# A hybrid transformer backbone on one core: no elementwise work on GpSimd in RWKV, a quota of products, source order on three engines, and weights two tiles ahead

## Chip, core and metric

The kernel runs on one core of a Trainium2 chip. The metric is the device time of one execution in microseconds (us); the time before is the median of three runs. The engines are TensorE (PE, with its weight loads PEld), VectorE (DVE), ScalarE (ACT), GpSimd (POOL) and SyncE (SP), which issues most transfers (DMAs); ScalarE issues some on a queue of its own (ACTq). Each engine runs its own instructions in order, and semaphores make one wait for another.

## The reference

Two layers work on 256 latent tokens and 256 context tokens of width 1024. Each is a feed-forward half step, three token mixers on one projection, and another feed-forward half step. Cut to what matters:

```python
z = _modulate(x, norm_g, m[3], m[4]) @ w_in             # all mixers' inputs and the gates zg
ya = attention(za)                                       # mixer A
yl = (lru(xl, forward) + lru(xl, reverse)) * gelu(ug)    # mixer B: gated linear recurrence
yr = head_groupnorm(o_forward + o_reverse + bonus) * gate  # mixer C: RWKV-7
g = sigmoid(zg)                                          # three gates of width 1024
acc = g[0] * (ya @ proj[0]) + g[1] * (yl @ proj[1]) + g[2] * (yr @ proj[2])
x = x + m[5] * (acc @ w_out)
```

RWKV runs, for each head and direction, `s = s * w + sa x (kk * a) + v x k`, with `sa = s . (-kk)`, over all tokens. In layer 1 only the latent half of the output is needed.

## The kernel before

Everything is float32. A product of weights is done in three parts: the weight tile (128 x 1024 of the matrix, loaded as `wr` on SP's queue) is cast to a short high half `wh` on ScalarE, the rest `wl = wr - wh` is subtracted on VectorE, and the input is split the same way (`h_hi`, `h_lo`, or `yh`, `yl`). `gemm_steps` then issues, for each of 8 blocks of 128 rows, the three products high x high, high x low and low x high: 24 products a tile, 512 columns each in layer 0 and 256 in layer 1 for the gates. `wload` does load, cast and subtraction in one go. In the stages named `r0` and `r1` a quarter of each tile's subtraction goes to GpSimd (`POOL_PART`).

The change lies in these two stages, about 600 to 1117 us (layer 0) and 2105 to 2560 us (layer 1). There, mixers B (`lru`) and C (`rwkv`) run beside the products of the rest of `w_in` (8 tiles for mixer B, 24 for the gates; `tiles`) and then the projections of branches 0 and 1 (`branch`, 96 products each): 960 products in all. `rwkv` works on four pairs of heads, called heads 0 to 3 here. Each goes through `direction` (decays, keys, and transposes `pt`), `decay`, `invert` (line 1160 begins it with the transposes `XZ`; `pq`, `pz`, `pm` and `pw` are its products), and `back` (`values`, `recur`).

The class `Weave` writes the order of PE. Each part is a generator that yields a `step` with its estimated cost on PE, VectorE, ScalarE and GpSimd and with what it needs. `run` keeps a model time: it takes the first part that is ready, and when none is, or PE was busy too little lately, it calls `fill` for one more product. The order of PE is that of the source in these stages (`manual_schedule`); the order on VectorE, ScalarE, GpSimd and SP is found by a scheduler, which may put an instruction far ahead of its place in the source.

`tiles` loads the tile after the present one before it issues the present one's products. A gate tile ends with a tanh on ScalarE (`gt`), stored to `gd`. `branch` loads its input in four tiles `yr` on ScalarE's queue (line 1450) and splits each as it comes (`yh` on ScalarE at line 231, `yl` on VectorE); `yr` has one buffer in layer 0 and two in layer 1. It then loads weights of `branch_proj` and the gates `gr` (line 1459, ScalarE's queue), issues products `bp`, and adds into `acc`. The transfer of `x` back from memory (line 1489, 2 MB in layer 0) is on ScalarE's queue too.

Of the kernel before, what the change touches and what calls it, by code (L numbers as in the profile page):

```python
# [8 lines left out]
F32 = mybir.dt.float32  # L9
# [18 lines left out]
HOP, BACKLOG, WINDOW, ACTIVE, PERIOD = 0.25, 1.5, 3.4, 3.3, 50.0  # L28
# [6 lines left out]
POOL_PART = {'r0': 0.25, 'r1': 0.25}  # L35
# [60 lines left out]
def build(tc, a, out, upto=99, dbg=None):  # L96
# [3 lines left out]
    with es:  # L100
# [90 lines left out]
        def wload(src, kt=KD, slot=None):  # L191

            n = wn[0]
# [4 lines left out]
            nc.sync.dma_start(out=view(raw), in_=src.rearrange("(k p) c -> p k c", p=P))  # L200
            if slot is None:
# [530 lines left out]
        class Weave:  # L732
# [13 lines left out]
            def products(self):  # L746
                if not self.fill(1):
                    return False
                self.busy(*self.product)
# [8 lines left out]
            def run(self, *parts):  # L758
# [4 lines left out]
                while at:  # L763
# [12 lines left out]
                    if best is None or (low and best[2][0]) or (wanted and self.t > self.owed):  # L776
                        if self.products():
# [5 lines left out]
                    pe, area, eng, lag, need = best[2]  # L783
                    self.busy(pe, area)
# [11 lines left out]
            owed = 0.0  # L796
# [4 lines left out]
        def lru(l, yd, done):  # L801
# [8 lines left out]
            def first(set_):  # L810
# [30 lines left out]
                for f in range(4):  # L841
# [4 lines left out]
                    yield step(dve=2.1, act=0.65, need=[("x", f)] + [("scanned", f - 2)] * (f > 1))  # L846
# [10 lines left out]
                    for d in range(2):  # L857
# [10 lines left out]
                        yield step(dve=0.7, act=1.95, pool=1.6)  # L868
                        nc.scalar.activation(tg[1], tg[1], AF.Identity, bias=one)
                        nc.gpsimd.tensor_tensor(bb[:, d], tg[1], xc, ALU.mult)  # L870
# [3 lines left out]
                    yield step(dve=1.4, act=1.3, pool=0.7, need=[("u", f)])  # L874
# [4 lines left out]
                    nc.gpsimd.tensor_scalar(w, w, 0.044715, 1.0, ALU.mult, ALU.add)  # L879
# [6 lines left out]
            def second(set_):  # L886
                for f in range(4):
# [3 lines left out]
                    for d in range(2):  # L891
                        yield step(pool=1.6, lag=1 - d)
                        nc.gpsimd.tensor_tensor(bb[:, d], th[:, d], bb[:, d], ALU.mult)
                    for d in range(2):
                        yield step(dve=1.3, lag=2)
# [8 lines left out]
                    yield step(dve=0.7, pool=1.6)  # L904
                    y = lp.tile([P, T], F32, tag="yl", name=f"yl{l}{f}", bufs=1)
                    nc.gpsimd.tensor_tensor(y[:, qc:], th[:, 0, qc:], th[:, 1, qc:], ALU.add)
# [44 lines left out]
        def rwkv(l, rk, z, zd, yd, weave, beside, before_last):  # L951
# [7 lines left out]
            with ExitStack() as ey:  # L959
# [4 lines left out]
                hv = rx.tile([P, 28], F32, tag="hv28", name=f"hv{l}")  # L964
                st, Y = {}, {}

                def setup():
# [7 lines left out]
                    nc.vector.tensor_scalar(hv[:, 24:28], hv[:, 20:24], -1.0, 1.0, ALU.mult, ALU.add)  # L975
                    nc.scalar.activation(twd, twd, AF.Tanh)
# [10 lines left out]
                    yield step(dve=4.5, act=0.4)  # L987
# [55 lines left out]
                def direction(f, d):  # L1043
                    nm = f"{l}{f}"

                    yield step(dve=1.22, pool=0.62, lag=0, need=[("tw", f)])
# [22 lines left out]
                    yield step(dve=1.4, pool=1.6 * d, lag=0, need=[("one", f)] * d + [("loaded", f)] * (f > 1))  # L1069
# [22 lines left out]
                def bonus(f):  # L1092

                    nm = f"{l}{f}"
                    yield step(dve=0.75, pool=1.15, lag=0, need=[("both", f)])
                    bon = st[f][4][0]

                    nc.gpsimd.tensor_copy(seg3(k_[f]), step_view(v_[f], 1))
# [28 lines left out]
                def decay(f, d):  # L1127

                    nm = f"{l}{f}"
                    yield step(pool=1.9, lag=0, need=[("paired", f, d)])  # L1130
# [252 lines left out]
                def finish(fs, pool):  # L1383

                    yield step(dve=4.5, act=0.4)
# [258 lines left out]
```

## Time and profile before

| what | value |
|---|---|
| median of three runs | 2797.81 us (2794.79 to 2802.01) |
| the profiled execution | 2800.25 us, its span 2798.4 us |
| mean granted clock of TensorE | 0.94 |
| PE busy | 2629.1 us (94%) |
| DVE busy | 1730.3 us (62%) |
| ACT busy | 1058.6 us (38%) |
| POOL busy | 406.7 us (15%) |

The span reaches from the first instruction to the last, and the time of the execution is a little longer. A busy share is a mean over the whole program: PE's 94% holds long stretches without a gap, and the two stages of the change, which hold most of the rest.

### The profile page before, as it was taken

What the parts mean: (1) busy time and instruction counts of PE and PEld (TensorE: products, weight loads), DVE (VectorE), ACT (ScalarE), POOL (GpSimd) and SP (SyncE); (2) the same over time, 40 slices, a digit from 0 to 9 for tenths busy, and PEclk for the clock granted to TensorE, in tenths of its full rate; (3) what the DMA queues carried; (4) which work ended last, traced back from release to release, by engine and by line L of the source; (5) the groups of instructions that cost most, each with busy time, mean ns of one, the idle gap of its engine ahead of it and who ended that gap; (6) DMA issues with size and microseconds to landing.
All of it is one profiled execution on the core that took longest, in us unless ns stands there. A gap on an engine that the chain in (4) does not pass through costs nothing. (4 is left out here: it accounts for less than half of the span.)

```text
span 2798.4 us, 47830 instructions
## 1 busy us (share of the span) xinstructions
PE 2629.1 (94%) x19761; PEld 2186.4 (78%) x19761; DVE 1730.3 (62%) x2934; ACT 1058.6 (38%) x1673; POOL 406.7 (15%) x381
## 2 busy tenths in 40 slices
PE   7999999997999999899999999999998899887899
PEld 5788888765677776798888978888776788777899
DVE  5867557657666644766655674555657656646565
ACT  4323233335544432332323432324346544333343
POOL 1000002224311102300000100001134432113000
PEclk9999999998898979999999999999999897768999
DMA  7646433122221125735443464544224331026465
GB/s 268 211 151 188 139 98 110 57 80 68 65 65 41 52 82 181 243 91 151 145 119 97 153 194 155 170 153 119 74 78 126 86 90 53 4 78 179 125 184 159
DMA packets 480092, 341.85 MB, mean 122 GB/s; under 512 B 17307, under 2 KB 448884, under 8 KB 479618
## 3 DMA queue, kind: packets, MB, share of 16 engines
q1 hardware_dynamic: 460690, 314.22, 37.2%
q10 hardware_dynamic: 19120, 24.52, 3.0%
q8 instruction: 155, 2.54, 0.4%
q14 instruction: 63, 0.52, 0.1%
q0 software_dynamic: 64, 0.05, 0.0%
HBM read 318.56 MB, written 20.19 MB: 121 GB/s over the span
## 5 line engine op out<-in xcount | busy, mean ns | idle before, releaser
L206 ACT CAST wh<-wr 128x1024 fp32r<-128x1024 f32 (+2 forms) x434 | 436.3, 1008 | 1079.0 <-PE gu L222 360.0
L215 DVE TENSOR_TENSOR wl<-wr,wh 128x1024 fp32r<-128x1024 f32 (+3 forms) x404 | 462.8, 1147 | 307.2 <-ACT wh L206 292.1
L222 PE MATMUL gu<-h_hi,wh 128*128 128x512 f32 (+1 forms) x1528 | 535.7, 352 | 6.2 <-ACT h_hi L388 2.6
L222 PE MATMUL gu<-h_hi,wl 128*128 128x512 f32 (+1 forms) x1528 | 534.0, 350 | 1.8 <-DVE wl L215 1.8
L222 PE MATMUL gu<-h_lo,wh 128*128 128x512 f32 (+1 forms) x1528 | 534.3, 350 | 0.7 <-DVE h_lo L389 0.5
L222 PE MATMUL win<-h_hi,wl 128*128 128x512 f32 (+1 forms) x896 | 335.0, 374 | 16.6 <-DVE wl L215 16.6
L222 PE MATMUL win<-h_hi,wh 128*128 128x512 f32 (+1 forms) x896 | 334.5, 374 | 1.1 <-ACT wh L206 0.6
L222 PE MATMUL win<-h_lo,wh 128*128 128x512 f32 (+1 forms) x896 | 332.6, 371 | 0.0
L222 PEld LDWEIGHTS gu<-h_hi,wh 128*128 128x128 f32 x1528 | 290.7, 191 | 49.8 <-ACT wh L206 6.3
L222 PEld LDWEIGHTS gu<-h_hi,wl 128*128 128x128 f32 x1528 | 291.4, 191 | 40.1 <-DVE wl L215 3.3
L222 PEld LDWEIGHTS gu<-h_lo,wh 128*128 128x128 f32 x1528 | 291.3, 191 | 37.5 <-DVE h_lo L389 1.5
L280 DVE SCALAR_TENSOR_TENSOR adacc<-adw,sc,adacc 128x1024 f32<-128x1024 f32 x196 | 245.1, 1286 | 6.0 <-ACT adacc L278 2.7
L222 PEld LDWEIGHTS win<-h_hi,wl 128*128 128x128 f32 x896 | 181.1, 202 | 57.4 <-issue 19.5
L222 PEld LDWEIGHTS win<-h_lo,wh 128*128 128x128 f32 x896 | 180.9, 202 | 36.6 <-issue 16.4
L222 PEld LDWEIGHTS win<-h_hi,wh 128*128 128x128 f32 x896 | 181.7, 203 | 32.6 <-issue 11.8
L222 PE MATMUL dn<-gh,wh 128*128 128x512 f32 (+1 forms) x560 | 200.8, 359 | 0.0
L222 PE MATMUL dn<-gl,wh 128*128 128x512 f32 (+1 forms) x560 | 199.4, 356 | 0.1
L222 PE MATMUL dn<-gh,wl 128*128 128x512 f32 (+1 forms) x560 | 199.4, 356 | 0.0
L214 POOL TENSOR_TENSOR wl<-wr,wh 128x256 fp32r<-128x256 f32 (+1 forms) x88 | 91.4, 1039 | 331.9 <-ACT wh L206 244.8
L290 POOL MEMSET adrow<- 128x256 f32 x18 | 5.6, 313 | 840.2 <-PE adt L297 840.2
L471 DVE SCALAR_TENSOR_TENSOR x<-dn,cf,x 128x256 f32<-128x256 f32 x120 | 53.6, 480 | 113.1 <-PE dn L222 112.8
L505 DVE TENSOR_TENSOR th<-th,gu 128x512 f32<-128x512 f32 (+1 forms) x88 | 54.4, 619 | 110.6 <-PE gu L222 110.4
(557 smaller groups left out, 4449.6 us busy)
## 6 DMA issues: line engine op xcount, KB each, us to landing
wr<-ffn_w_gu SPq DMA_DIRECT2D x176, 512.0 KB
adw<-ada_w SPq DMA_DIRECT2D x144, 512.0 KB
wr<-w_in SPq DMA_DIRECT2D x106, 512.0 KB
wr<-ffn_w_d SPq DMA_DIRECT2D x64, 512.0 KB
wr<-ffn_w_d SPq DMA_DIRECT2D x35, 384.0 KB
wr<-w_out SPq DMA_DIRECT2D x17, 512.0 KB
gd<-gt SPq DMA_DIRECT2D x24, 256.0 KB
wr<-branch_proj SPq DMA_DIRECT2D x24, 256.0 KB
```

The source lines that it names most:

```text
L206: nc.scalar.copy(hi[:, 0:w], raw[:, 0:w])
L214: nc.gpsimd.tensor_tensor(lo[:, m:w], raw[:, m:w], hi[:, m:w].bitcast(F32), ALU.subtract)
L215: eng.tensor_tensor(lo[:, 0:m], raw[:, 0:m], hi[:, 0:m].bitcast(F32), ALU.subtract)
L222: nc.tensor.matmul(ps[:, c0:c1], wt[:, k], xt(k)[:, c0:c1], start=(k == 0 and j == 0), stop=(k == kt - 1 and j == 2))
L280: nc.vector.scalar_tensor_tensor(acc, w, f, acc, ALU.mult, ALU.add)
L290: nc.gpsimd.memset(row, 0.0)
L471: nc.vector.scalar_tensor_tensor(x[:, k, cs], ps[:, cs], coef[:, s, k:k + 1], x[:, k, cs], ALU.mult, ALU.add)
L505: nc.vector.tensor_tensor(th[:, c0:], th[:, c0:], pp[1][:, c0:], ALU.mult)
```

## The change

The change has four parts, all of them in the two stages.

1. *GpSimd.* All elementwise work of the stages leaves GpSimd: the quarter of `wl` and the operations on `bb`, `yl`, `km` go to VectorE (the first, `bb`, as one fused operation, for which ScalarE loses an addition), and `gl`, `tw`, the copy of `v` and the decay go to ScalarE, the decay as eight activations of 128 columns. Memsets stay.
2. *Quota.* `Weave` refuses a product when more than 960 x (0.08 + steps / 390) are sent, unless one is wanted. The modelled hop is 0.3 instead of 0.25 us, and the costs of some steps are new.
3. *Order.* `manual_schedule` covers VectorE and ScalarE as well: their instructions stand as the source has them, the transfers that ScalarE issues included.
4. *Transfers.* `tiles` fetches a tile of `w_in` two tiles ahead; its cast and subtraction stand after product 9 of 24 of the tile before. `branch` is not changed.

```diff
-HOP, BACKLOG, WINDOW, ACTIVE, PERIOD = 0.25, 1.5, 3.4, 3.3, 50.0
+HOP, BACKLOG, WINDOW, ACTIVE, PERIOD = 0.3, 1.5, 3.4, 3.3, 50.0
+STEPS, PRODUCTS, AHEAD = 390, 960, 0.08
-POOL_PART = {'r0': 0.25, 'r1': 0.25}
+POOL_PART = {}
...
-            def products(self):
+            def products(self, wanted=False):
+
+                if not wanted and self.sent > PRODUCTS * (AHEAD + self.steps / STEPS):
+                    return False
                 if not self.fill(1):
                     return False
+                self.sent += 1
...
-                        nc.scalar.activation(tg[1], tg[1], AF.Identity, bias=one)
-                        nc.gpsimd.tensor_tensor(bb[:, d], tg[1], xc, ALU.mult)
+                        nc.vector.scalar_tensor_tensor(bb[:, d], tg[1], 1.0, xc, ALU.add, ALU.mult)
...
-                    nc.gpsimd.tensor_scalar(w, w, 0.044715, 1.0, ALU.mult, ALU.add)
+                    nc.scalar.activation(w, w, AF.Identity, bias=one, scale=0.044715)
...
-                        nc.gpsimd.tensor_tensor(bb[:, d], th[:, d], bb[:, d], ALU.mult)
...
+                        nc.vector.tensor_tensor(bb[:, d], th[:, d], bb[:, d], ALU.mult)
...
-                    nc.gpsimd.tensor_tensor(y[:, qc:], th[:, 0, qc:], th[:, 1, qc:], ALU.add)
+                    nc.vector.tensor_tensor(y[:, qc:], th[:, 0, qc:], th[:, 1, qc:], ALU.add)
...
-                    nc.gpsimd.tensor_scalar(tw, tw, -0.5 * E05, -0.5 * E05, ALU.mult, ALU.add)
+                    nc.scalar.activation(tw, tw, AF.Identity, bias=hv[:, 28:29], scale=-0.5 * E05)
...
-                        nc.gpsimd.tensor_tensor(seg3(bon)[:, s0:], seg3(bon)[:, s0:], step_view(km, 1)[:, s0:], ALU.add)
+                        nc.vector.tensor_tensor(seg3(bon)[:, s0:], seg3(bon)[:, s0:], step_view(km, 1)[:, s0:], ALU.add)
...
-                    nc.gpsimd.tensor_copy(seg3(k_[f]), step_view(v_[f], 1))
+                    nc.scalar.copy(seg3(k_[f]), step_view(v_[f], 1))
...
-                    nc.gpsimd.tensor_tensor(bkT[:, d], bkT[:, d], pc[:, d, :, None].to_broadcast([P, NCH, P]), ALU.mult)
+                    for j in range(NCH):
+                        nc.scalar.activation(bkT[:, d, j], bkT[:, d, j], AF.Copy, scale=pc[:, d, j:j + 1])
...
+            fetch = lambda t: t and wfetch(a["w_in"][l][:, t[0] * P:(t[0] + 1) * P])
+            now, then = following(), following()
+            w, raw = wsplit(fetch(now)), fetch(then)
             while now:
                 i, c0, key = now
-                now = following()
-                wn_ = load(now[0]) if now else None
+                last = following()
+                ahead = fetch(last)
...
+                for n, _ in enumerate(gemm_steps(ps, w, lambda k: h_hi[:, k], lambda k: h_lo[:, k], KD, c0)):
+                    yield
+                    if n == 8 and then:
+                        wn_ = wsplit(raw)
...
-                with tc.manual_schedule(engines={mybir.EngineType.PE}):
+                with tc.manual_schedule(engines={mybir.EngineType.PE, mybir.EngineType.DVE, mybir.EngineType.Activation}):
```

`wfetch` is the first half of `wload` (the transfer), `wsplit` the second (cast and subtraction). In the following rows, a row is a line, an operation and `output<-inputs`; the numbers are those of the program's tiles.

ScalarE in layer 0, where branch 0 is prepared, before: `gt` is a gate's tanh, `yr` a load, `yh` its cast, `gr` a load of a gate.

```order
L1436 ACTIVATE gt_8959<-win_48_8861 128x512
L1450 DMA yr_9399<-yd_3754 128x512
L1273 COPY W_6333<-pu_8977 64x512 x2
L1273 COPY W_6333<-pu_8988 64x512 x2
L1273 COPY W_6333<-pu_9000 64x512 x2
L555 CAST hvo_9011<-hvo_9011 128x128
L1273 COPY W_6333<-pu_9036 64x512 x2
L231 CAST yh_9397<-yr_9399 128x512
L1459 DMA gr_9422<-gd_3757 128x512
L1459 DMA gr_9424<-gd_3757 128x512
L1286 COPY ar_7955<-pM_9055 128x3x64
L1450 DMA yr_9403<-yd_3754 128x512
```

ScalarE at the same work, after; `win_52` is the last tile of `w_in`.

```order
L1407 ACTIVATE z_1_4908<-z_1_4908,vb_2241 128x512
L1407 ACTIVATE zr_2_7019<-zr_2_7019,vb_2241 128x512
L1452 ACTIVATE gt_9341<-win_52_9156 128x512
L1466 DMA yr_9346<-yd_3754 128x512
L239 CAST yh_9344<-yr_9346 128x512
L1466 DMA yr_9350<-yd_3754 128x512
L239 CAST yh_9344<-yr_9350 128x512
L1466 DMA yr_9354<-yd_3754 128x512
L239 CAST yh_9344<-yr_9354 128x512
L1466 DMA yr_9358<-yd_3754 128x512
L239 CAST yh_9344<-yr_9358 128x512
L214 CAST wh_9364<-wr_9362 128x512
```

Before, the loads of branch 0 stand among the products of the tiles `win_48` and on; after, all four loads and casts stand behind the `gt` of the last tile, and the first weight cast behind them.

ScalarE in layer 0, before, where the last loads of branch 1 (`yr` from `yd_3755`) stand and `x` comes back:

```order
L1450 DMA yr_9618<-yd_3755 128x512
L231 CAST yh_9604<-yr_9618 128x512
L555 CAST hvo_9339<-hvo_9339 128x128
L1450 DMA yr_9822<-yd_3756 128x512
L206 CAST wh_9428<-wr_9426 128x512
L1436 ACTIVATE gt_9394<-win_52_9365 128x512
L1394 ACTIVATE zr_3_7940<-zr_3_7940,vb_2241 128x512
L206 CAST wh_9456<-wr_9454 128x512
L1459 DMA gr_9452<-gd_3757 128x512
L1489 DMA x_9819<-xd_3761 128x4096
L1459 DMA gr_9475<-gd_3757 128x512
```

The same, after:

```order
L1407 ACTIVATE zr_3_8017<-zr_3_8017,vb_2241 128x512
L1466 DMA yr_9615<-yd_3755 128x512
L239 CAST yh_9613<-yr_9615 128x512
L1505 DMA x_9820<-xd_3761 128x4096
L1466 DMA yr_9619<-yd_3755 128x512
L239 CAST yh_9613<-yr_9619 128x512
L1466 DMA yr_9623<-yd_3755 128x512
L239 CAST yh_9613<-yr_9623 128x512
L1466 DMA yr_9627<-yd_3755 128x512
L239 CAST yh_9613<-yr_9627 128x512
L214 CAST wh_9633<-wr_9631 128x512
```

The transfer of `x` stood behind the loads of branch 1, and stands now behind the first of the four.

PE in layer 1 around `pq` of head 2, before:

```order
L1246 MATMUL pa_20770<-ident,ar_20257 64x128 x8
L534 MATMUL oss_20781<-z_5_17056,sel 32x128 x2
L1246 MATMUL pa_20785<-ident,ar_20257 64x128 x8
L1187 MATMUL pq_20796<-XZ_20629,bt_20258 32x16 x64
L1256 MATMUL pm_20862<-W_19308,bt_20258 64x64 x16
L1256 MATMUL pm_20881<-W_19308,bt_20258 64x64 x16
L564 MATMUL hbk_20906<-hrsk_18147,selT 128x512
L1026 MATMUL ptw_20914<-z_12_17256,wup_17877 128x512
```

and after:

```order
L1259 MATMUL pa_20735<-ident,ar_19937 64x128 x8
L1200 MATMUL pq_20746<-XZ_20507,bt_19938 32x16 x64
L230 MATMUL win_51_20733<-h_lo,wh_20694 128x256
L230 MATMUL win_51_20733<-h_hi,wl_20695 128x256
L230 MATMUL win_51_20733<-h_hi,wh_20694 128x256
L230 MATMUL win_51_20733<-h_lo,wh_20694 128x256
L230 MATMUL win_51_20733<-h_hi,wl_20695 128x256
L1269 MATMUL pm_20817<-W_19131,bt_19938 64x64 x16
L230 MATMUL win_51_20733<-h_hi,wh_20694 128x256
L230 MATMUL win_51_20733<-h_lo,wh_20694 128x256
```

No product of a weight tile stood around `pq` of head 2; now products of `win_51` do.

## Rows read from the trace of the kernel before

**Rows 1.** Windows of layer 0: us, busy time by engine, PEclk the granted clock.

```profile
610.00:710.00 100.00, 82.42 (x378) 57.45 (x378) 72.74 (x141) 49.17 (x72) 36.36 (x34) 0.89 0.28 77
...
770.00:1060.00 290.00, 287.27 (x3760) 218.20 (x3758) 171.13 (x327) 115.17 (x191) 45.81 (x45) 0.90 0.21 61
```

**Rows 2.** Waits of PE, 610 to 760 us: total us, times, longest.

```profile
PE lg L863 <- DVE xc L856: 9.0, 3, 3.6
```

**Rows 3.** Windows of layer 1, cut where a head begins its inversion.

```profile
2105.00:2203.00 98.00, 78.77 (x474) 61.78 (x473) 66.71 (x122) 56.10 (x83) 42.64 (x42) 0.90 0.42 116
2203.00:2305.00 102.00, 94.86 (x1202) 82.19 (x1202) 67.02 (x111) 57.31 (x88) 37.04 (x36) 0.90 0.30 88
2305.00:2373.00 68.00, 63.23 (x948) 55.98 (x945) 43.97 (x84) 30.45 (x53) 14.67 (x15) 0.77 0.18 56
2373.00:2439.00 66.00, 54.75 (x942) 46.64 (x941) 42.80 (x91) 24.38 (x44) 9.86 (x9) 0.74 0.02 4
```

**Rows 4.** Waits of PE, 2105 to 2265 us.

```profile
PE win L222 <- DVE wl L215: 16.0, 6, 5.1
```

**Rows 5.** Waits of PE, 2330 to 2480 us.

```profile
PE pq L1187 <- DVE XZ L1172: 12.0, 2, 6.0
...
PE bp L222 <- ACT yh L231: 5.0, 2, 3.7
```

**Rows 6.** GpSimd by line, 2100 to 2560 us: busy us, mean ns.

```profile
L214 POOL TENSOR_TENSOR wl<-wr,wh 128x256 fp32r<-128x256 f32 x40 | 45.4, 1137 | 112.9 <-ACT wh L206 88.6 <-ACT ar L1286 7.7 <-DVE XZ L1167 5.6
L1133 POOL TENSOR_TENSOR bt<-bt,pc 128x1024 f32<-128x1024 f32 x8 | 15.2, 1896 | 40.6 <-PE pt L1119 40.6
```

**Rows 7.** VectorE by line, 2100 to 2560 us, the low half of a tile.

```profile
L215 DVE TENSOR_TENSOR wl<-wr,wh 128x768 fp32r<-128x768 f32 x40 | 40.6, 1020 | 26.0 <-ACT wh L206 24.7 <-POOL acc L1477 0.9 <-ACT ar L1286 0.3
...
L215 DVE TENSOR_TENSOR wl<-wr,wh 128x1024 fp32r<-128x1024 f32 x5 | 7.1, 1426 | 1.8 <-ACT wh L206 1.8
```

**Rows 8.** Line 1169 in 2105 to 2310 us: duration in ns, least, median, most.

```profile
L1169 DVE TENSOR_TENSOR XZ<-XZ x14: 192/256/1402, 2207.7 to 2227.6; 64x28 f32<-64x28 f32 x2, 64x52 f32<-64x52 f32 x2, 64x72 f32<-64x72 f32 x2, 64x88 f32<-64x88 f32 x2
```

**Rows 9.** Timeline of PE in layer 0: start us, duration us, instruction.

```profile
1064.01 0.39 PE L222 MATMUL win<-h_hi,wh 128*128 128x512 f32 x1
1064.23 0.39 PE L222 MATMUL win<-h_lo,wh 128*128 128x512 f32 x1
```

**Rows 10.** Timeline of ScalarE and its queue (ACTq), layer 0.

```profile
1047.55 0.33 ACTq L1450 DMA_DIRECT2D yr<-yd  x1
1052.62 0.62 ACT L231 CAST yh<-yr 128x512 fp32r<-128x512 f32 x1 [6.68 <-DMA yr<-yd]
1054.00 0.33 ACTq L1450 DMA_DIRECT2D yr<-yd  x1
...
1063.56 0.33 ACTq L1450 DMA_DIRECT2D yr<-yd  x1
1066.70 0.62 ACT L231 CAST yh<-yr 128x512 fp32r<-128x512 f32 x1 [2.87 <-DMA yr<-yd]
1067.86 0.30 ACT L555 CAST hvo<-hvo 128x128 fp32r<-128x128 f32 x1 [0.54 <-DVE hvo L553]
```

**Rows 11.** Window that holds the load of x in layer 0.

```profile
1078.00:1088.00 10.00, 9.20 (x40) 7.05 (x38) 3.09 (x5) 1.24 (x2) 1.30 (x2) 1.00 0.96 350
```

**Rows 12.** Timeline of ScalarE and its queue, layer 1.

```profile
2472.21 0.86 ACTq L1450 DMA_DIRECT2D yr<-yd  x2
...
2475.41 0.40 ACT L231 CAST yh<-yr 128x256 fp32r<-128x256 f32 x1 [2.63 <-DMA yr<-yd]
...
2476.69 0.82 ACTq L1450 DMA_DIRECT2D yr<-yd  x2
...
2479.01 0.40 ACT L231 CAST yh<-yr 128x256 fp32r<-128x256 f32 x1 [1.17 <-DMA yr<-yd]
```

**Rows 13.** Windows behind an idle stretch of PE, after layer 1's stage.

```profile
2592.00:2598.00 6.00, 1.95 (x6) 1.14 (x6) 3.81 (x18) 0.91 (x2) 0.00 (x0) 0.50 0.20 61
2598.00:2604.00 6.00, 6.00 (x32) 6.00 (x32) 5.38 (x13) 2.72 (x6) 0.00 (x0) 0.53 0.01 3
```

More of the change, by code (lines that the diff above doesn't have):

```diff
@@ L191, in wload, with wfetch @@
         def wload(src, kt=KD, slot=None):
+            return wsplit(wfetch(src, kt), kt, slot)
+        def wfetch(src, kt=KD):
             n = wn[0]
@@ L200, in wload, with wsplit @@
             nc.sync.dma_start(out=view(raw), in_=src.rearrange("(k p) c -> p k c", p=P))
+            return raw, w, n, view
+        def wsplit(fetched, kt=KD, slot=None):
+            raw, w, n, view = fetched
             if slot is None:
@@ L776, in run @@
                     if best is None or (low and best[2][0]) or (wanted and self.t > self.owed):
-                        if self.products():
+                        if self.products(wanted):
                             self.owed = self.t + self.product[0]
@@ L783, in run @@
                     pe, area, eng, lag, need = best[2]
+                    self.steps += 1
                     self.busy(pe, area)
@@ L794, in run @@
                         at.remove(best)
-            owed = 0.0
+            owed, sent, steps = 0.0, 0, 0
         tile_of, read = {}, [0]
@@ L891, in second @@
                     for d in range(2):
-                        yield step(pool=1.6, lag=1 - d)
-                        nc.gpsimd.tensor_tensor(bb[:, d], th[:, d], bb[:, d], ALU.mult)
-                    for d in range(2):
-                        yield step(dve=1.3, lag=2)
+                        yield step(dve=2.0, lag=1 - d)
+                        nc.vector.tensor_tensor(bb[:, d], th[:, d], bb[:, d], ALU.mult)
                         A, B, H = aa[:, d], bb[:, d], th[:, d]
@@ L963, in rwkv @@
                 wup, aup = (rx.tile([P, T], F32, tag=n, name=f"{n}{l}") for n in ("wup", "aup"))
-                hv = rx.tile([P, 28], F32, tag="hv28", name=f"hv{l}")
+                hv = rx.tile([P, 29], F32, tag="hv29", name=f"hv{l}")
                 st, Y = {}, {}
@@ L975, in setup @@
                     nc.vector.tensor_scalar(hv[:, 24:28], hv[:, 20:24], -1.0, 1.0, ALU.mult, ALU.add)
+                    nc.vector.memset(hv[:, 28:29], -0.5 * E05)
                     nc.scalar.activation(twd, twd, AF.Tanh)
@@ L986, in setup @@
                         head_rows(pss, sq, f, 0, lambda q: f == 0, f == 3)
-                    yield step(dve=4.5, act=0.4)
+                    yield step(dve=6.5, act=0.4)
                     st["rsK"] = head_rsqrt(rx, rt, "tw0", pss, 0, 1.0, 1e-24, ALU.max, f"k{l}")
@@ L1068, in direction @@
                     nc.vector.tensor_tensor(bt[:, 0, d, :, 1], ta.rearrange("p (j t) -> p j t", t=CH), iP, ALU.mult)
-                    yield step(dve=1.4, pool=1.6 * d, lag=0, need=[("one", f)] * d + [("loaded", f)] * (f > 1))
+                    yield step(dve=1.4 + 0.7 * d, lag=0, need=[("one", f)] * d + [("loaded", f)] * (f > 1))
                     kks = step_view(kk, d).rearrange("p s (j t) -> p s j t", t=CH)
@@ L1383, in finish @@
                 def finish(fs, pool):
-                    yield step(dve=4.5, act=0.4)
+                    yield step(dve=6.5, act=0.4)
                     rsO = head_rsqrt(pool, pool, "hvo", Y["oss"], qc // P, 1.0 / 64, 64e-5, ALU.add, f"o{l}{fs[0]}")
@@ L1423, in following @@
                 return gates.pop(0) if gates else None
-            load = lambda i: wload(a["w_in"][l][:, i * P:(i + 1) * P])
-            now = following()
-            w = load(now[0])
+            fetch = lambda t: t and wfetch(a["w_in"][l][:, t[0] * P:(t[0] + 1) * P])
+            now, then = following(), following()
+            w, raw = wsplit(fetch(now)), fetch(then)
             while now:
                 i, c0, key = now
-                now = following()
-                wn_ = load(now[0]) if now else None
+                last = following()
+                ahead = fetch(last)
                 gate = isinstance(key, int)
                 ps = (mmt if gate else cht)(f"win{l}_{i}")
-                yield from gemm_steps(ps, w, lambda k: h_hi[:, k], lambda k: h_lo[:, k], KD, c0)
+                for n, _ in enumerate(gemm_steps(ps, w, lambda k: h_hi[:, k], lambda k: h_lo[:, k], KD, c0)):
+                    yield
+                    if n == 8 and then:
+                        wn_ = wsplit(raw)
                 if gate:
@@ L1439, in tiles @@
                     done[key], tile_of[key] = 0.0, ps
-                w = wn_
+                now, then, w, raw = then, last, wn_, ahead
         def branch(l, b, mp, acc, yd, gd):
```

15 lines of the change are left out of this document (8 added, 7 removed).

## The prediction

> **What bounds the kernel now.** I read the busy time of each engine in stretches of the two RWKV stages first, then what TensorE (PE) waited for there, then the instructions of the engines that the change touches. The change moves instructions in these two stages alone (layer 0 from about 600 to 1117 us, layer 1 from about 2105 to 2560 us); outside them the order of every engine is as it was. In layer 0 the stage is bound by PE: it is busy for 287.3 of the 290 us from 770 to 1060, and idle for 17.6 of the 100 us from 610 [rows 1]. The largest wait of those is for the convolution on VectorE, 9.0 us [rows 2]. Layer 1 is different. Its four heads begin their inversion at about 2203, 2305, 2373 and 2439 us, and the stretches between them hold 19.2, 7.1, 4.8 and 11.2 us of PE idle time, the last two at a granted clock of 0.77 and 0.74 [rows 3]. Early in the stage PE waits 16.0 us for the low half of a weight tile [rows 4]; late in it, where the products of `w_in` have run out, 12.0 us for `XZ` before `pq` [rows 5]. So there is something to win: 17.6 us early in layer 0, the 19.2 and 7.1 us of the first two stretches of layer 1, and the late waits.
>
> **GpSimd emptied.** In layer 1 alone its quarter of the weight tiles cost 45.4 us in 40 pieces and the decay 15.2 us in 8 [rows 6]. VectorE takes the quarter: a tile of 1024 columns takes it 1426 ns where 768 took 1020 [rows 7], so 40 x 0.41 = 16 us in layer 1 and about 13 us for the 32 tiles of layer 0. The other moved operations (`bb` twice for each of eight, `km`, `yl`) are some 24 instructions at about 0.7 us for 512 columns, which is half of that 1426 ns: 11 to 16 us. VectorE gains some 27 us of work a layer. It gets part back: the same small product `XZ` took 192 ns at best and 1402 ns at worst [rows 8], and the long ones stood where GpSimd worked too. I take 15 us back a layer. ScalarE gets the decay as 8 pieces of 128 columns, at 0.30 us each by the cast of that size [rows 10], so 2.4 us for 1.9 us on GpSimd, and the bias, copy and `gl` operations; with 56 of 98 us busy in its fullest stretch [rows 3] it holds that, and I cost it at nothing; the work of VectorE and PE beside it is its cover. Were that gone, two decays a head would add 2 x 2.4 = 4.8 us a head.
>
> The Trainium skill, "SBUF — State Buffer", section "Who interferes with whom", says that the port pair which VectorE and GpSimd share is locked for a whole instruction, so that one blocks the other. The rows of `XZ` agree (192 against 1402 ns). By that rule nearly all of the VectorE time that I book as added would come back, and the first rival below would be likelier than I make it.
>
> **Two tiles ahead.** The split of the next tile now stands after product 9 of 24, and its fetch a tile earlier. In the early stage of layer 1 this, with the chain through GpSimd gone (the wait for `wl` is 16.0 us [rows 4]), should take most of the waits: I take 12 of the 19.2 us, since VectorE has 66.7 of 98 us of work there already [rows 3] and gets more. In layer 0 I take somewhat over half of 17.6, 10 us.
>
> **The quota.** Counted in the order of PE, the products issued between one head's `pq` and the next's were, in layer 1, 394, 266, 20 and 0; they become 266, 170, 198 and 47. A product of 512 columns in layer 0 starts 0.22 us after the last one [rows 9]; layer 1 has 256 columns, so about 0.11 us. Heads 0 and 1 lose 14.1 and 10.6 us of PE work; heads 2 and 3 get 19.6 and 5.2. The late stretches hold 4.8 + 11.2 us of idle time and run at a clock of 0.77 and 0.74 [rows 3], so they can take most of the 24.8 us without growing. The early two shrink by at most 24.7 us; where VectorE or the chain of a head sets the pace they don't shrink at all, and products taken away there uncover waits. I take 12 won early and 4 lost late: -8 us, between -25 and +10. In layer 0 the counts move little (201, 180, 101, 100 against 226, 193, 109, 109) and I cost that at nothing.
>
> Gains: 10 + 12 + 8 = 30 us, of at most some 17.6 + 19.2 + 24.7 = 62.
>
> **The order of the source on ScalarE.** This is where I expect the loss. `branch` loads its four tiles `yr` on ScalarE's own queue, and each load is followed in the source by the cast that waits for it. Before, the order found for ScalarE put the loads of branch 0 in layer 0 far ahead, between other work, at a time when PE still had products of `w_in`: the view of PE's waits from 1010 to 1060 us is empty. After, ScalarE's rows read: `gt` of the last tile of `w_in`, then load, cast, load, cast four times, then the cast of the first weight tile. `gt` needs the last product of `w_in`, and the very next row of PE, the first product of branch 0, needs that weight cast: nothing on PE covers the chain. Behind the waiting casts everything else of ScalarE is queued, the `gr` loads and later weight casts too, and VectorE's subtractions `yl` behind them.
>
> Its price: from the issue of a load to the start of its cast 5.07 us (1047.55 to 1052.62) and 3.14 us (1063.56 to 1066.70), and 1.38 us from there to the next issue, since layer 0 has one buffer for `yr` (1052.62 to 1054.00) [rows 10]. Four loads, three such steps, the last cast and the weight cast at 0.62 each: 4 x L + 4.1 + 1.2, which is 17.9 us at 3.14 and 25.6 at 5.07. I take 19, near the lower row, as other traffic is light then. For **branch 1** of layer 0 the chain is the same, with one more transfer in it: the 2 MB load of `x` stands on the same queue between the first `yr` and the second, and at the 350 GB/s of the stretch that holds it before [rows 11] it takes 6 us. ScalarE can run about two tiles of 12 products at 0.22 us [rows 9] ahead of PE there, 5.3 us. I take 16 us, between 8 and 24. In **layer 1** L was 3.20 us (2472.21 to 2475.41) and 2.32 us (2476.69 to 2479.01) [rows 12]; two loads went out together before, one by one now. Four times L, four casts of 0.40 [rows 12] and a weight cast of twice 0.62: 12.1 to 15.6 us, where PE waited 5.0 before [rows 5]. I take +9 for branch 0 and +4 for branch 1, which has heads' work to cover it. Sum: 19 + 16 + 9 + 4 = 48 us, between 30 and 65.
>
> The Trainium skill, "DMA: Bandwidth & Descriptors", section "Anatomy of one DMA", gives 2.0 us plus bytes over 436 GB/s, 2.6 us for these 256 KB (it is stated for another issue path); the rows show 3.14 and more. By it the first chain would be 15.7 us. Its "Rules for kernel authors" want a load issued early and waited for late, which speaks against this order.
>
> **The clock.** After an idle stretch PE ran at 0.50 and 0.53 of full speed for two stretches of 6 us, busy in 1.95 and 6.00 us of them [rows 13]. Two long stalls, each followed by some 7 us of work at half clock, lose 3.5 us each: 7 us, between 0 and 14.
>
> **Sum.** 48 + 7 - 30 = +25 us on the profiled 2800.25 us, 2825. That execution lies 2.4 us over the median of 2797.81, so the time to expect is 2823.
>
> **Rivals.**
> 1. *The gains win.* The chains at the branch starts hide or are short (under 5 us each, 12 together), and emptying GpSimd gives VectorE all its time back. For it: 1402 against 192 ns [rows 8], and 16 us of waits for `wl` [rows 4]. Against it: the chain in layer 0 has nothing on PE beside it. Then -45 + 12 = -33: 2765. It decides if the wait of the first `bp` in layer 0 is below 5 us.
> 2. *Cancelled.* Stalls of 35 us, as the loads land in 2.3 us throughout, against gains of 35: 2798.
> 3. *VectorE becomes the bound.* It carries some 27 us more a layer with no 15 us returned; in the first two stretches of layer 1 (66.7 of 98 and 67.0 of 102 us busy [rows 3]) the order in source stops it from working past a wait. From about 85 us of work in one of them it sets the pace: the gains fall to 10 and the stalls stay: +45, 2843. For it: VectorE's order is now fixed too. Against it: it still has 30 us free in each.
> 4. *The quota does nothing*, as the stretches 2 and 3 grow by what 0 and 1 lose. That is -22 + 55 = +33: 2831, inside my range.
>
> **How the numbers follow.** About 0.3% (8.4 us) is what a measurement of this kernel can tell from no change. The forecast with rival 4: 0.54; rival 1: 0.18; rival 2: 0.14; rival 3: 0.14. Rival 1 is the only one faster, and I give it 0.2 with the edge of rival 2; slower takes the forecast and rival 3, some 0.66. The range goes from 2780, stalls of 30 against gains of 48, to 2856, stalls and clock of 68 against gains of 10. The lower part of rival 1 is left out, and the upper of rival 3.
>
> **What would show it.** In the profile after: `bp` on PE waits some 18 us for the weight cast on ScalarE or its `yh` at the start of branch 0 in layer 0, some 15 at branch 1, some 12 in layer 1; the granted clock falls to 0.50 behind. PE's idle time in the first 160 us of either stage halves. In layer 1, win products stand beside `pq` of head 2 and the `XZ` waits fall. GpSimd's busy time falls from 406.7 us to about 200. I am wrong if the casts `yh` start back to back, or if VectorE is busy for nine tenths of head 0 or 1.

## Result and the profile after

The changed kernel takes 2881.89 us (median; 2880.32 to 2883.45) against 2798.64 us before: a ratio of 1.030, 95% interval 1.028 to 1.0316, 83 us slower. The forecast was 25 us slower. Its direction was right, its size was not: the range ended at 2856.

The stalls that the prediction rests on are there. Waits of TensorE in the changed kernel, the longest in each of four stretches that hold the start of one branch, in the columns of [rows 2]; `bp` is a product of a branch:

```profile
PE bp L230 <- ACT wh L214: 18.3, 1, 18.3
...
PE bp L230 <- ACT wh L214: 19.3, 1, 19.3
...
PE bp L230 <- ACT wh L214: 11.7, 1, 11.7
...
PE bp L230 <- ACT wh L214: 7.8, 1, 7.8
```

Against the 5.0 us of [rows 5] and the 3.0 us that branch 1 waited for `yh` in layer 1 before, this is 18.3 + 19.3 + 6.7 + 4.8 = 49 us, where 48 were forecast. ScalarE's timeline shows the chain as it was worked out; these are the rows that answer to [rows 10], load and cast in turn:

```profile
1064.41 0.34 ACTq L1466 DMA_DIRECT2D yr<-yd  x1
1067.61 0.62 ACT L239 CAST yh<-yr 128x512 fp32r<-128x512 f32 x1 [2.63 <-DMA yr<-yd]
1068.98 0.33 ACTq L1466 DMA_DIRECT2D yr<-yd  x1
1072.30 0.62 ACT L239 CAST yh<-yr 128x512 fp32r<-128x512 f32 x1 [4.07 <-DMA yr<-yd]
1073.67 0.33 ACTq L1466 DMA_DIRECT2D yr<-yd  x1
...
1121.01 0.33 ACTq L1505 DMA_DIRECT2D x<-xd  x1
1121.67 0.33 ACTq L1466 DMA_DIRECT2D yr<-yd  x1
1129.34 0.62 ACT L239 CAST yh<-yr 128x512 fp32r<-128x512 f32 x1 [8.43 <-DMA yr<-yd]
```

In these rows a load takes 3.2 to 3.3 us from issue to cast, the step to the next issue takes 1.37 us, and the load behind that of `x` takes 7.7 us.

What is missing is the gain. Windows of the two kernels, before first (columns as in [rows 1]). In layer 0 they are cut at the end of `w_in`'s products and at the end of branch 1, in layer 1 at the start of branch 0:

```profile
600.00:1070.00 470.00, 442.74 (x4771) 329.76 (x4769) 291.60 (x559) 206.90 (x328) 108.71 (x100) 0.89 0.23 68
1070.00:1150.00 80.00, 73.30 (x304) 55.95 (x305) 42.94 (x62) 21.83 (x36) 30.05 (x30) 0.98 0.67 203
...
2105.00:2475.00 370.00, 316.13 (x4128) 268.77 (x4127) 241.81 (x457) 178.31 (x284) 105.10 (x102) 0.82 0.23 67
```

```profile
600.00:1065.00 465.00, 433.15 (x4701) 324.09 (x4699) 281.28 (x540) 224.45 (x385) 7.18 (x18) 0.90 0.20 60
1065.00:1195.00 130.00, 83.46 (x355) 59.95 (x356) 57.54 (x96) 27.94 (x47) 21.93 (x15) 0.83 0.52 152
...
2150.00:2535.00 385.00, 322.43 (x4130) 267.92 (x4129) 243.75 (x472) 201.10 (x355) 5.25 (x15) 0.83 0.22 61
```

Up to the end of `w_in` layer 0 is 5 us shorter, where 10 were forecast; with the branches it is 45 us longer. In layer 1 the stretch up to branch 0 is 15 us longer, where 20 us of gain were forecast. Layer 1's last window, which holds its branches, grew by 20 us. PE's idle time did not halve: it is 31.9 us up to the end of `w_in` in layer 0, after 27.3. In layer 1 the stretches of heads 0 and 1, cut as in [rows 3], hold 28.4 and 17.0 us of it, after 19.2 and 7.1, and together they are not shorter (203 us after 200):

```profile
2150.00:2251.00 101.00, 72.56 (x401) 52.74 (x401) 65.48 (x132) 58.25 (x94) 0.22 (x2) 0.85 0.31 83
2251.00:2353.00 102.00, 85.05 (x1099) 72.45 (x1099) 64.92 (x117) 54.45 (x94) 3.06 (x7) 0.82 0.19 55
```

There the wait for `wl` fell as forecast, from the 16.0 us of [rows 4] to 5.4. But PE now waits longer for other work of VectorE, the convolution `xc` above all; waits from 2100 to 2310 us:

```profile
PE lg L876 <- DVE xc L869: 14.6, 3, 6.8
...
PE win L230 <- DVE wl L223: 5.4, 4, 4.0
```

From the first section of the page after, GpSimd is at 191.2 us, as forecast:

```profile
PE 2638.3 (92%) x19761; PEld 2186.9 (76%) x19761; DVE 1741.5 (60%) x2984; ACT 1107.3 (38%) x1817; POOL 191.2 (7%) x197
```

### The profile page after: what moved, and what is told of

Read it like the earlier page. It is cut to its first block, busy times and chain, and to the rows that moved or that the text cites. A ratio compares the mean times of both kernels' runs of the same rounds, so it can differ in the third digit from the quotient of the medians.

```text
span 2881.0 us, 47640 instructions
## 1 busy us (share of the span) xinstructions
PE 2638.3 (92%) x19761; PEld 2186.9 (76%) x19761; DVE 1741.5 (60%) x2984; ACT 1107.3 (38%) x1817; POOL 191.2 (7%) x197
## 5 line engine op out<-in xcount | busy, mean ns | idle before, releaser
L223 DVE TENSOR_TENSOR wl<-wr,wh 128x1024 fp32r<-128x1024 f32 (+2 forms) x404 | 476.2, 1181 | 352.3 <-ACT wh L214 351.1
L230 PE MATMUL bp<-yh,wh 128*128 128x512 f32 (+1 forms) x192 | 73.0, 382 | 77.1 <-ACT wh L214 66.3
L230 PEld LDWEIGHTS dn<-gh,wh 128*128 128x128 f32 x560 | 105.2, 188 | 16.8 <-ACT wh L214 1.3
```

The costliest lines, as they stand in the source:

```text
L223: eng.tensor_tensor(lo[:, 0:m], raw[:, 0:m], hi[:, 0:m].bitcast(F32), ALU.subtract)
L230: nc.tensor.matmul(ps[:, c0:c1], wt[:, k], xt(k)[:, c0:c1], start=(k == 0 and j == 0), stop=(k == kt - 1 and j == 2))
```

## The experiments

The theory was that the order of the source on ScalarE stalls PE at the branch starts (A); the rivals, that the other parts cost the time (B), or that the order also holds back the heads (C). Each ratio is to the kernel before, run on the same chip beside it, since the median of that one was between 2787 and 2799 us from chip to chip.

### Which part: the order

**Order of the source on TensorE alone** (`e_order_pe`):

```diff
-with tc.manual_schedule(engines={mybir.EngineType.PE, mybir.EngineType.DVE, mybir.EngineType.Activation}):
+with tc.manual_schedule(engines={mybir.EngineType.PE}):
```

> The changed kernel with the order of the source on TensorE alone, as before the change; VectorE and ScalarE are ordered by the scheduler again. Theory A (the order on ScalarE puts the loads of the branches behind their casts and stalls TensorE at four branch starts): the 46 us of waits of bp in layer 0 after 1060 us and some 15 us in layer 1 go, and the time falls from 2882 to about 2815. Theory B (emptying GpSimd and the quota cost the time, order is secondary): it stays at 2860 or more.

2763.32 us, 0.991 (0.987 to 0.995). Everything in the change but the order is a gain of 0.9%, and the order costs 118 us (2881.89 - 2763.32; by the ratios 0.039 x 2798 = 109). Theory B is out; A is too small, as 2763 is 52 us below the 2815 that it gave. Windows of this kernel, cut at the same two places of layer 0:

```profile
600.00:1025.00 425.00, 412.83 (x4684) 310.07 (x4684) 280.83 (x547) 226.02 (x391) 6.83 (x18) 0.96 0.24 71
1025.00:1110.00 85.00, 78.00 (x377) 57.95 (x376) 48.77 (x91) 24.61 (x43) 22.19 (x16) 0.98 0.65 202
```

Layer 0 is 40 us shorter than before, and the part up to the end of `w_in` 45 us, in two ways. The idle time falls from 27.3 to 12.2 us, and the granted clock rises from 0.89 to 0.96. Busy time times the clock is 394 us before and 396 here, about the same work. By this estimate 49 of the 443 busy us went to the clock before, and 17 here. In the changed kernel the clock is back at 0.90 and the idle time at 31.9 us.

**VectorE, or ScalarE, in the order of the source**: `e_order_pe_dve` leaves ScalarE to the scheduler, `e_order_pe_act` VectorE.

```diff
+with tc.manual_schedule(engines={mybir.EngineType.PE, mybir.EngineType.DVE}):
...
+with tc.manual_schedule(engines={mybir.EngineType.PE, mybir.EngineType.Activation}):
```

> The changed kernel with ScalarE alone ordered by the scheduler again; VectorE keeps the order of the source. Theory A: about 2815 to 2825, as the loads yr go ahead again and only what VectorE's order costs is left. If VectorE's order is what holds the heads of layer 1 back (about 20 us), 2835.

> The changed kernel with VectorE alone ordered by the scheduler again; ScalarE keeps the order of the source. Theory A: the stalls at the branch starts stay (four casts of yr, each behind its load, 19 us in layer 0), so 2865 to 2885. If VectorE's order is the main cause instead, 2825 or less.

2840.25 us, 1.018 (1.014 to 1.023), and 2853.46 us, 1.023 (1.019 to 1.027). Either order alone costs most of it, 77 and 90 us over `e_order_pe`. Waits of PE in layer 0, VectorE's order first, then ScalarE's:

```profile
PE bp L230 <- DVE wl L223: 30.8, 4, 18.4
```

```profile
PE bp L230 <- ACT wh L214: 39.9, 7, 18.7
```

The prediction's sum had only ScalarE in view. VectorE in a fixed order stands at `yl`, which needs the cast `yh` of the same load, with `wl` behind it. PE waits 11.3 us for that `wl` at branch 0 and 18.4 at branch 1, where it waited 18.3 and 19.3 in the changed kernel. VectorE at branch 0 in `e_order_pe_dve`:

```profile
1055.53 0.69 DVE L240 TENSOR_TENSOR yl<-yr,yh 128x512 fp32r<-128x512 f32 x1 [3.61 <-ACT yh L239]
1056.14 1.29 DVE L223 TENSOR_TENSOR wl<-wr,wh 128x512 fp32r<-128x512 f32 x2
```

**The order added to the kernel before** (`e_before_order`), with GpSimd's work and without quota and the second tile ahead; the edit is that of `manual_schedule` in the change.

> The kernel before with one part of the change, the order of the source on VectorE and ScalarE; GpSimd's work, no quota and the fetch of one tile ahead stay. Theory C: the order alone costs about as much as it did beside the other parts, 85 to 120 us, so 2880 to 2915. If the order is dear only because VectorE has GpSimd's work too: 2840 or less.

2841.77 us, 1.020 (1.0175 to 1.022): 53 us on that chip. Here the sum is of the size that theory A gives: all waits of `bp` for `wh` are 37.9 us in layer 0 and 19.3 in layer 1, 57 us. Counted in the same way they are 45.8 and 20.5 us in the changed kernel, 9 us more, yet there the order costs twice as much. The forecast for the order, 48 + 7 us, is close to what the order costs the kernel before.

```profile
PE bp L222 <- ACT wh L206: 37.9, 9, 17.9
...
PE bp L222 <- ACT wh L206: 19.3, 3, 11.7
```

**Layer 1 alone** (`e_order_layer1`):

```diff
+with tc.manual_schedule(engines={mybir.EngineType.PE} | ({mybir.EngineType.DVE, mybir.EngineType.Activation} if l else set())):
```

> The changed kernel with the order of the source on VectorE and ScalarE in layer 1 alone; in layer 0 on TensorE alone. By the places of the two profiles, the order loses some 82 us in layer 0 and 31 in layer 1, so 2763 + 31 = 2794. If a late layer 0 had helped layer 1 or the reverse, the parts don't add: below 2780 or above 2810.

2791.48 us, 1.0017 (0.9999 to 1.0035), 28 us above `e_order_pe`. So the order costs about 28 us in layer 1. The windows of layer 0 differ by 85 us (595 after, 510 in `e_order_pe`), and the two add up to the whole; the order in layer 0 alone was not run.

### What the other parts are worth, with a free order

**GpSimd emptied alone** (`e_pool_alone`): as `e_order_pe`, with one tile ahead and a quota that never binds; the planner's new step costs stay. **Without the quota** (`e_pe_no_quota`), **with one tile ahead** (`e_pe_one_ahead`), and **with a quarter of each tile's `wl` back on GpSimd** (`e_pe_pool_part`):

```diff
-STEPS, PRODUCTS, AHEAD = 390, 960, 0.08
+STEPS, PRODUCTS, AHEAD = 390, 960, 8.0
...
-            w, raw = wsplit(fetch(now)), fetch(then)
+            w = wsplit(fetch(now))
...
-POOL_PART = {}
+POOL_PART = {'r0': 0.25, 'r1': 0.25}
```

> The kernel before with GpSimd emptied and the planner's new step costs alone: order of the source on TensorE only, no quota, weights fetched and split one tile ahead as before. If emptying GpSimd is what brings the 1.0% that all parts but the order bring: a ratio of 0.990 to the kernel before. If the fetch of two tiles ahead brings it: 1.000. If the forecast's DVE load (27 us a layer) weighs: above 1.005.

> The changed kernel with the order of the source on TensorE alone and without the quota. If the quota gives part of the 29 us that this kernel gains with it: about 2785. If the gain is GpSimd's and the quota gives nothing: 2763. If the quota costs, as in the pair with the order of the source (2849 against 2882): 2740.

> The changed kernel with the order of the source on TensorE alone and with weights one tile ahead as before; GpSimd emptied, quota kept. If two tiles ahead matter: 0.998 or more against 0.991 with them; if not: 0.990 to 0.992.

> The changed kernel with the order of the source on TensorE alone and with a quarter of each weight tile's subtraction back on GpSimd; its other work stays off. If GpSimd beside VectorE slows VectorE: 2775 to 2785, with long instances of small VectorE operations back. If VectorE's extra 13 to 16 us a layer weigh more: 2755.

`e_pool_alone` takes 2749.31 us, 0.986 (0.982 to 0.990), the lowest of all: 45 us less than before on that chip, and less than the changed kernel by 4%. With the second tile ahead added it is 2756.0, 0.989 (0.986 to 0.992); with the quota added instead 2755.93, 0.988 (0.984 to 0.992); with both 0.991. So with a free order neither the quota nor the second tile gains anything, and the intervals overlap too much to say that they lose. The quarter of `wl` on GpSimd gives 2772.1, 0.9945 (0.992 to 0.997), some 9 us more than without it, which the intervals hardly tell apart. Why GpSimd's work was so dear, the longest operation of [rows 8] shows. It ends within 0.1 us of the operation that GpSimd ran beside it, in the kernel before:

```profile
2207.69 1.40 DVE L1169 TENSOR_TENSOR XZ<-XZ 64x28 f32<-64x28 f32 x1
...
2207.77 1.28 POOL L870 TENSOR_TENSOR bb<-tg,xc 128x512 f32<-128x512 f32 x1
```

The same line in `e_pool_alone`, over both layers, and with the quarter of `wl` back on GpSimd (`e_pe_pool_part`):

```profile
L1182 DVE TENSOR_TENSOR XZ<-XZ x112: 169/241/269, 705.5 to 2406.4; 64x28 f32<-64x28 f32 x16, 64x52 f32<-64x52 f32 x16, 64x72 f32<-64x72 f32 x16, 64x88 f32<-64x88 f32 x16
...
L1182 DVE TENSOR_TENSOR XZ<-XZ x112: 151/243/793, 701.2 to 2427.1; 64x28 f32<-64x28 f32 x16, 64x52 f32<-64x52 f32 x16, 64x72 f32<-64x72 f32 x16, 64x88 f32<-64x88 f32 x16
```

The longest instance is 269 ns with GpSimd emptied, 793 with a part of its work back, and 1402 before. And the first section of the page of `e_pool_alone`:

```profile
PE 2604.4 (95%) x19761; PEld 2171.8 (79%) x19761; DVE 1730.3 (63%) x2984; ACT 1107.8 (40%) x1817; POOL 190.7 (7%) x197
```

VectorE is busy for 1730.3 us, as it was before (1730.3 us), with 50 more instructions, and with all that it took over from GpSimd (what went to ScalarE is not in it): the 27 us a layer, as the prediction estimates them, came back whole. In `e_pe_pool_part` GpSimd has some 29 us of it back (13 and 16 us by the prediction's estimate), and VectorE is not busy for less: 1735.5 us, where `e_order_pe` has 1729.0.

### Where the order costs more than the branch starts

**The loads of a branch written earlier** (`e_yr_early`), one load or cast after every fourth product of the tiles ahead, all in the order of the source:

```diff
+        def prepare(l, b, mp, yd, ready):
...
+                nc.scalar.dma_start(out=yr, in_=yd[b][:, f, qc:])
+                yield
+                yield
+                split(yh[:, f], yl[:, f], yr)
+                yield
...
+                            tick[0] += 1
+                            if tick[0] % 4 == 0 and side:
+                                next(side[0], None)
```

> The changed kernel, with VectorE and ScalarE in the order of the source as there, but with the four loads of a branch's input and their casts written earlier in the source, one step after every fourth product of the tiles before. Theory A (the branch starts are most of the order's cost): the two stalls of 19 us in layer 0 fall to about 6 and 2 us, the time to about 2835. Theory C (the order of the source also holds back the heads of RWKV): about 2835 too, but 70 us stay above the run whose order is free, with waits in the heads. If the loads were no cause at all: 2880.

2850.97 us, 1.023 (1.020 to 1.0265). In layer 0 the waits of `bp` for `wh` fall from 45.8 us to 17.8, and branch 1 ends 22 us earlier. In layer 1 the wait at branch 0 stays at 11.7 us, since no product of a tile is left ahead of it:

```profile
PE bp L230 <- ACT wh L214: 17.8, 9, 5.9
```

The branch starts are shown as a cause, for 22 us of the forecast 35 in layer 0. Some 88 us above `e_order_pe` stay: 42 of them in layer 0 before branch 0 (the last product of `w_in` begins at 1068 us here, at 1026 there).

**Candidates for the rest.** Each gate's tanh written behind product 9 of the next tile (`e_yr_gt`); the first ten products and two splits ahead of the setup of the mixers (`e_start`); no quota (`e_yr_no_quota`), all three on `e_yr_early`; and no quota in the changed kernel itself (`e_no_quota`):

```diff
-                if gate:
+                    if n == 8:
+                        if later:
+                            later.pop()()
...
+                    weave.sent += fill(10)
...
-STEPS, PRODUCTS, AHEAD = 390, 960, 0.08
+STEPS, PRODUCTS, AHEAD = 390, 960, 8.0
```

> The kernel with the loads of the branches written earlier (order of the source on three engines), and with each gate's tanh written behind product 9 of the next tile instead of behind its own last product. Theory D: ScalarE stands at that tanh until TensorE has come there (18.8 and 11.1 us in layer 0), and what is queued behind it holds the heads back: 15 to 25 us less, a ratio near 1.015 after 1.023. If the blocking comes from other instructions: 1.023.

> The kernel with the loads of the branches written earlier (order of the source on three engines), and with the first ten products of the stage, with the split of the first two tiles, written ahead of the setup of the mixers B and C. Theory E: the subtraction wl stands behind a row of 30 small operations of the setup on VectorE, and this start costs 7.6 us of TensorE's idle time in layer 0 and 7 in layer 1: 8 to 15 us less, a ratio of 1.016 after 1.023. If the start is made up later by the planner's slack: 1.021 to 1.023.

> The kernel with the loads of the branches written earlier (order of the source on three engines), without the quota. If the quota is dear under the order of the source, as the pair of 1.030 with it and 1.0225 without said, and independent of the branch starts: a ratio near 1.015. If that pair differed by the branch starts alone: 1.023.

> The changed kernel without the quota: its bound is never reached, all else stays. If the quota is what lost 18 us between the first head's inversion and the last's in layer 1: about 2864. If the quota helps there as forecast (8 us): about 2890. The stalls at the branch starts stay in both.

`e_yr_gt`: 2846.46 us, 1.020 (1.0165 to 1.024), which its interval can't tell from 1.023, so theory D gets no support. `e_yr_no_quota`: 2844.84 us, 1.020 (1.016 to 1.025), the same. `e_no_quota`: 2849.06 us, 1.0225 (1.018 to 1.027), against 1.030 with the quota: the quota costs some 20 us in the changed kernel, and nothing that can be told where the loads stand earlier. `e_start`: 2871.38 us, 1.031 (1.027 to 1.035), slower. The start of the stage was a real stall of the changed kernel, seen in VectorE's timeline: the first subtraction `wl` stands behind the row of small operations `sv` that runs from 619.87 to 625.18 us.

```profile
624.82 0.17 DVE L847 TENSOR_TENSOR sv<-sv 128x8 f32<-128x8 f32 x1
625.02 0.17 DVE L848 TENSOR_SCALAR sv<-sv 128x8 f32<-128x8 f32 x1
625.11 0.16 DVE L849 TENSOR_SCALAR sv<-sv 128x8 f32<-128x8 f32 x1
625.18 0.17 DVE L852 TENSOR_SCALAR gb<-vb 128x16 f32<-128x16 f32 x1
625.25 2.35 DVE L223 TENSOR_TENSOR wl<-wr,wh 128x1024 fp32r<-128x1024 f32 x2
```

With the edit head 0 begins its inversion 5 us earlier in layer 0 (703.1 us, 708.3 in `e_yr_early`). But branch 1 ends 6 us later there, and layer 1 loses more: theory E is right on the spot and wrong on the time. Why the edit makes it slower stays open.

**GpSimd emptied, with the order** (`e_pool_order`, `e_pool_alone` with the order added), and the changed kernel with one group of operations back on GpSimd: the quarter of `wl` (`e_back_wl`), what went to ScalarE (`e_back_act`), the small ones that went to VectorE (`e_back_dve`). One line of each:

```diff
+with tc.manual_schedule(engines={mybir.EngineType.PE, mybir.EngineType.DVE, mybir.EngineType.Activation}):
...
+POOL_PART = {'r0': 0.25, 'r1': 0.25}
...
+nc.gpsimd.tensor_tensor(bkT[:, d], bkT[:, d], pc[:, d, :, None].to_broadcast([P, NCH, P]), ALU.mult)
...
+nc.gpsimd.tensor_tensor(bb[:, d], th[:, d], bb[:, d], ALU.mult)
```

> The kernel with GpSimd emptied alone (0.986 of the kernel before), with the order of the source on VectorE and ScalarE added; no quota, one tile ahead. Order added to the kernel before costs 53 us, to all other parts of the change 118. If it is GpSimd's work on VectorE and ScalarE that makes the order dear: about 2750 + 95 = 2845 or more. If it is the quota or the split after product 9: 2750 + 55 = 2805.

> The changed kernel with the order of the source on three engines, and the quarter of each weight tile's subtraction back on GpSimd. Theory F: VectorE's longer row in a fixed order is what makes the order dear, and the largest piece of it, 13 to 16 us a layer, gives back 15 to 30 us: a ratio of 1.020 to 1.025 after 1.030. If the order is dear by its waits and not by VectorE's load: 1.028 to 1.032.

> The changed kernel with the order of the source on three engines, and what went from GpSimd to ScalarE (the decay, tw, gl, the copy of v) back on GpSimd. If ScalarE's row is what makes the order dear: 20 us or more less, 1.023 or below. If not: 1.028 to 1.032.

> The changed kernel with the order of the source on three engines, and the small elementwise work that went from GpSimd to VectorE (bb twice, yl, km, with ScalarE's addition) back on GpSimd. If these operations, which in a fixed order stand before the work of the heads, hold the heads back: 20 us or more less, 1.023 or below. If not: 1.028 to 1.032.

`e_pool_order`: 2876.67 us, 1.032 (1.027 to 1.037), 127 us above `e_pool_alone`. So the order is dear with the emptied GpSimd and the step costs that go with it, whether or not quota and second tile are there; that tile gains some 27 us here (1.032 without it, 1.0225 in `e_no_quota` with it, the intervals just apart). But no group of the operations by itself makes it dear: back on GpSimd, `wl` gives 2882.39 us, 1.034 (1.0315 to 1.036), ScalarE's 2889.97, 1.038 (1.036 to 1.039), VectorE's 2892.41, 1.037 (1.035 to 1.040), all at or above the 1.030 of the change. Theory F falls. All three groups back at once were not tried.

A mark of the fixed order is seen in each kernel that has it on ScalarE. How long VectorE stood in layer 0, from 600 to 1060 us, at a subtraction `wl` for the cast `wh`, in the columns of [rows 2]: before, the change, and `e_order_pe`.

```profile
DVE wl L215 <- ACT wh L206: 21.9, 9, 9.1
```

```profile
DVE wl L223 <- ACT wh L214: 54.6, 15, 12.0
```

```profile
DVE wl L223 <- ACT wh L214: 19.2, 12, 5.3
```

It is 58.0 us in `e_before_order`, 55.1 in `e_yr_early`, 16.9 in `e_order_pe_dve`, where ScalarE is free, and 11.1 in `e_pool_alone`. In a fixed order the work of the heads stands behind each of these waits. As it is as long in `e_before_order`, where the order costs half, it doesn't explain the difference by itself.

The first sections of the pages say where the difference lies, `e_before_order` first, then `e_pool_order`:

```profile
PE 2615.1 (92%) x19761; PEld 2175.3 (77%) x19761; DVE 1736.3 (61%) x2934; ACT 1057.8 (37%) x1673; POOL 411.3 (14%) x381
...
PE 2646.3 (92%) x19761; PEld 2194.8 (76%) x19761; DVE 1741.2 (61%) x2984; ACT 1107.1 (38%) x1817; POOL 190.8 (7%) x197
```

PE's idle time is the span less its busy time. The order takes it from 169 to 225 us in the kernel before (span 2840.5 us with it), and from 142 to 230 us in `e_pool_alone` (spans 2746.1 and 2875.9). So under the fixed order PE stands idle as long with GpSimd emptied as with its work: the 28 us of idle time that emptying wins with a free order are gone. PE's busy time, for the same 19761 products, falls by 14 us in the first pair and rises by 42 in the second, where the mean granted clock falls from 0.949 to 0.931. These are single executions, and those of the kernel before lie up to 27 us apart, so the split is rough. **What stays open** is why the fixed order costs some 70 us more with GpSimd emptied, the clock's part above all: whether by the planner's new order of steps, which the emptied kernels share, or by many small waits of the two engines on each other. Undoing the step costs alone was not tried.

## Why the prediction was wrong

- **The stalls at the branch starts: right.** 49 us against 48 for the longest wait at each of the four, by the chain as worked out; the first 18.3 us (19 forecast), the load behind `x` 7.7 us.
- **The clock after them: right.** The window from 1065 to 1195 us, which holds the two stalls of layer 0, has a granted clock of 0.83, where the answering one before had 0.98. Busy time at less than full clock, summed over steps of 1 us, costs 6.7 us there by estimate and 1.7 before: 5 us for the two stalls, where 7 were forecast.
- **The step that failed is the order's price outside the branch starts.** The prediction costed VectorE's order at nothing and ScalarE's at the four chains with the clock behind them, 55 us, and took off gains of 30 us worked out for engines that may still reorder. In the changed kernel the order costs 109 to 118 us. With a free order the other parts do gain 0.9%, about 26 us; with the order fixed this gain is gone, and 25 to 30 us more. So gains and stalls don't add; that both go through what stands behind a wait on VectorE and ScalarE is the likely reason, not a shown one. The sum of +25 is what the order and the other parts give apart: 53 - 26 = +27. That the 30 came so near 26 is luck, as its parts were wrong.
- **Emptying GpSimd was mis-sized.** The prediction returned 15 of 27 us a layer to VectorE; all came back, and alone it gains 1.4% with a free order. The Trainium skill, "SBUF — State Buffer", section "Who interferes with whom", states the lock for a whole instruction for VectorE's 2-port modes; of an operation with two inputs in SBUF, as `XZ` is, it says that it contends with a GpSimd instruction that reads SBUF. The trace agrees that it contends: the longest instance fell from 1402 to 269 ns.
- **The clock of layer 0 was missed.** "Bound by PE" was read from the busy time, 287.3 of 290 us. But that row has a clock of 0.90 [rows 1], and something was to be won there: of the 45 us by which `e_order_pe` shortens layer 0 up to the end of `w_in`, 30 are busy time.
- **The quota and the second tile were mis-sized:** forecast 8 and 22 us of gain; with a free order neither shows any. In the change's order the quota costs some 20 us and the second tile gains some 27, and the two early stretches of layer 1, which were to shrink, are as long as before (203 us after 200).
- **The rivals.** Rival 1 describes the kernel with the order left free, not the change; that this one took 2763 us against its 2765 is luck, as rival 1 still held 12 us of stalls. Rival 3 (2843 us) came nearest in time, and its words on a fixed order point the right way. Its mechanism did not come: VectorE was busy for 65.5 of 101 and 64.9 of 102 us in the stretches of heads 0 and 1 of layer 1, not nine tenths.

## What to carry to other kernels

An order written by a planner for one engine is not an order for the engines that feed it. Where theirs is fixed, every load has to stand well ahead of the instruction that waits for it, and even that gave back only a part here. Test the order apart from the other edits, since it can swallow their gains. Work on GpSimd wasn't free for VectorE here, so look at the spread of a small operation's duration before counting such work as parallel. Read busy time beside the granted clock: a stretch that is 99% busy at 0.9 can hold as much to win as one with idle time.

## What the runs showed of the hardware

Some 50 us of VectorE's busy time over two stages went with GpSimd's work, by the prediction's estimate of what moved: VectorE took over that much from GpSimd, and its total stayed at 1730.3 us. And a busy PE is not a PE at full clock. Windows of the changed kernel in layer 0:

```profile
772.00:776.00 4.00, 0.00 (x0) 0.00 (x0) 3.88 (x5) 0.00 (x0) 0.00 (x0) 0.50 0.00 0
...
788.00:792.00 4.00, 4.00 (x33) 3.23 (x31) 0.00 (x0) 1.66 (x3) 0.00 (x0) 0.50 0.02 4
...
848.00:852.00 4.00, 4.00 (x148) 3.40 (x148) 3.92 (x5) 0.00 (x0) 0.00 (x0) 1.00 0.32 104
...
856.00:860.00 4.00, 4.00 (x36) 3.40 (x33) 0.60 (x1) 1.16 (x2) 0.00 (x0) 0.50 0.02 4
```

The clock fell to 0.50, half of full speed, while PE stood idle, and it was still there from 788 to 792 us, with PE busy throughout. From 856 to 860 us it was 0.50 again, without any idle time since 780 us; just before it PE had run 128 products of 16 columns:

```profile
849.81 2.20 PE L1200 MATMUL pq<-XZ,bt 16*32 16x16 f32 x128
```

That these small products brought the clock down is not shown; no run here took them out.
